# Moving the nine steps of the delta rule's inverses one row later in a hybrid decoder trunk

## The chip, the cores and the metric

The kernel runs on one core of a Trainium2 chip. A core has TensorE (matrix products, which write to PSUM), VectorE, ScalarE and GpSimd (elementwise work) and SyncE, whose queue issues the DMA transfers here. The metric is device time in microseconds; a time is the median of several runs, and one more execution is recorded by the hardware profiler. In the profile's rows PE is TensorE, PEld its weight loads, DVE VectorE, ACT ScalarE, POOL GpSimd and SPq the queue of SyncE.

## The reference

Two decoder layers over 512 tokens of width 1024, in float32. Each layer normalises x, projects it once, and feeds three branches: a Mamba-2 state space scan (SSD), multi-head latent attention (MLA) and a gated delta rule (GDN). Each branch is projected to the model width and multiplied by a sigmoid gate made from the same normalised x; the sum goes through an output projection, and a squared-ReLU feed-forward block follows.

```
g_ssd, g_mla, g_gdn = jnp.split(gates, N_BRANCH, axis=-1)
mixed = g_ssd * (y_ssd @ w_ssd_out) + g_mla * (y_mla @ w_mla_out) + g_gdn * (y_gdn @ w_gdn_out)
h = x + mixed @ w_out
f = jnp.square(jax.nn.relu(rmsnorm(h, norm2_g) @ w_up)) @ w_down
```

The delta rule has 8 value heads in chunks of 64 tokens. Each chunk and head needs the solution of a unit lower triangular system, which is what "the inverses" are:

```
a_mat = jnp.where(strict, jnp.einsum('bhcld,bhcmd->bhclm', kb, k) * decay, 0.0)
sol = lax.linalg.triangular_solve(a_mat + jnp.eye(L, dtype=jnp.float32), rhs, left_side=True, lower=True)
```

## The kernel before

**Products.** A float32 product is made of three matmuls in a faster format: each operand is split into a high part and the remainder. For weights, `split_half` casts the raw tile to `whi` on ScalarE (L154) and subtracts on VectorE to get `wlo` (L155); `mm3` issues the three matmuls (L182 to L184). Raw weights arrive by DMA into two buffers `wraw` (L161), issued by SyncE; `whi` and `wlo` have four buffers each.

**Rows.** `dense_F` makes 256 columns of a projection of K = 1024. Its weights come in four pieces, each of two 128-deep slices by 256 columns. One piece gives twelve matmuls of 128x512 (two output tiles, two slices, three matmuls each) into two of four PSUM banks `acc`. Such a piece is called a row here. Behind each row `dense_F` calls the function `after`, if it was given one.

**The state space projection.** `out_proj` goes through four pairs of output tiles. For each pair it makes the gate product (four rows on `xh`, `xl`, the normalised input) and the branch product (four rows on `yh`, `yl`). The projection of the state space branch is `out_proj(a["w_ssd_out"][ly], 0, ...)`; it has 32 rows, counted 0 to 31 here. Its `after` is `between`, which counts the rows and, from a given number on, runs one of a list of steps behind each row. The same `between` is also given to the query product (`key_tiles` in `gdn_unit`, four rows), so that steps left over run there: these are the counts 32 to 35 for the first unit.

**The inverses.** The 128x128 blocks of the delta rule for two units of four heads (tiles `nt`, tag `tok`) are made by `gdn_matrix`. Then:

- `gdn_blocks` inverts the 32x32 diagonal blocks on VectorE in 31 dependent pairs of operations (L879, L880), transposes the result (L882), writes both forms to memory (`d_x`, `d_y`, L885) and reads them back in another layout into the tiles `wk0` to `wk3` (L888: `wk<-d_x` for both units, then `wk<-d_y` for both). It is written ahead of the projection, and its VectorE work runs while the projection's early rows run on TensorE.
- `gdn_inverse` returns nine steps that put the inverses together: `first(0)`, `first(1)`, `second(0)`, `second(1)` and `last_doubling(0)` to `last_doubling(4)`. `first(u)` copies the block inverses (L907, L908 on ScalarE) and issues 64 small matmuls of 32x32 (L913), which read the tiles `wk<-d_x`. `second(u)` has 96 small matmuls (L929, L930). `last_doubling(i)` has up to sixteen of 64x64 (L949 of one half, L951 of the half before), whose results VectorE and ScalarE copy (L954, L956). Each step needs the copies of earlier ones. The small products go to three PSUM banks `sm`.

`gdn_unit(u)` then makes queries (convolved by L687 on ScalarE and L691 on VectorE), values and gates of a unit, and runs the scan over the chunks, which is the first to read the finished inverses.

**Order.** Nothing waits by hand. The program is written as one sequence; a planner orders each engine's instructions by a simulated clock: of those whose data and buffers it believes to be there, the one written first goes first (some are raised by `tc.high_priority`). So an instruction may stand later in its engine's queue than where it was written, when the planner believes its data to be late. At run time each engine, and SyncE's queue, takes its instructions strictly in the planned order and waits on semaphores.

Of the kernel before, what the change touches and what calls it, by code (L numbers as in the profile page):

```python
# [55 lines left out]
def hybrid_kernel(ctx, tc, a, out, depth=2, taps=None):  # L56
# [294 lines left out]
    for ly in range(depth):  # L351
# [609 lines left out]
        def gdn_unit(u, kT, ork, cc, cd, Yt, yh, yl):  # L961
            hd0 = 16 + 4 * u
            qT = key_tiles(2 * u, between)
            pss = sm_bank()
            for i in range(2):
# [116 lines left out]
        steps = gdn_inverse([m[4] for m in mats], blocks)  # L1082

        rows = itertools.count()

        def between():
            if next(rows) >= 24 and steps:
                steps.pop(0)()

        out_proj(a["w_ssd_out"][ly], 0, *ys, br, after=between)  # L1090
        yg = hilo_tags(lp, "y")
        for u in range(2):
# [302 lines left out]
```

## Time and profile before

| what | us |
|---|---|
| median of three runs | 2314.41 |
| the three runs | 2310.45, 2318.05, 2314.41 |
| profiled execution, its own time | 2314.88 |
| span of the profiled execution | 2313.1 |
| TensorE busy | 2272.7 |
| VectorE busy | 1647.6 |
| ScalarE busy | 1200.5 |

The span goes from the first to the last instruction; the execution's own time also has what lies around it, 1.78 us here. The profile gives for each engine its busy time, for groups of instructions their count, mean duration and idle time before them with what ended it, and a chain of work followed back from the last instruction. Matmuls are pipelined: the printed duration of one overlaps the next, so the pitch from start to start says what one costs. The mean granted clock of TensorE was 0.998. Each of the two layers goes once through the stage of the change: the first near 500 us and the second near 1646 us in the trace.

### The profile page before, as it was taken

How to read it: one execution, taken by the hardware profiler on the slowest of the kernel's cores; microseconds unless marked ns; L12 is line 12 of the kernel's file. 1: busy time of each engine (PE TensorE's matmuls, PEld its weight loads, DVE VectorE, ACT ScalarE, POOL GpSimd, SP SyncE). 2: the span in 40 equal slices, each digit the busy share in tenths (PEclk: the TensorE clock that was granted, in tenths of full speed). 3: DMA queues.
4: the chain of work that ended last, by engine and by line, in shares of the span. 5: the costliest groups of instructions: out<-in, count | busy, mean ns of one | idle time of the engine just before them, and what ended most of it. 6: DMA issues, size and time to landing. Idle time of an engine off the chain costs nothing.

```text
span 2313.1 us, 32290 instructions
## 1 busy us (share of the span) xinstructions
PE 2272.7 (98%) x11810; PEld 1866.7 (81%) x11810; DVE 1647.6 (71%) x3256; ACT 1200.5 (52%) x2509; POOL 59.5 (3%) x74
## 2 busy tenths in 40 slices
PE   9999999999999999999999999999999999999998
PEld 8788787878887888888888887878788878888886
DVE  7777566876667768767867775668657668778668
ACT  6766644333443455554657666433334435645545
POOL 0000000000000000000000000000000000000000
PEclk9999999999999999999999999999999999999999
DMA  4223534452324243233122236334422241433231
GB/s 142 80 74 101 191 101 119 125 140 74 87 69 164 65 146 107 94 104 108 59 89 79 75 107 197 95 112 141 119 82 83 65 164 55 160 107 101 89 110 46
DMA packets 220032, 244.16 MB, mean 106 GB/s; under 512 B 34256, under 2 KB 172384, under 8 KB 219872
## 3 DMA queue, kind: packets, MB, share of 16 engines
q1 hardware_dynamic: 219872, 242.09, 34.1%
q8 instruction: 93, 1.52, 0.3%
q14 instruction: 67, 0.55, 0.1%
HBM read 225.60 MB, written 11.74 MB: 103 GB/s over the span
## 4 chain that ended last, share of the span: by engine, by line
PE 86%; DVE 8%; ACT 2%; DMA 2%; POOL 1%; issue 1%; SPq 0%; DVEq 0%; POOLq 0%; ACTq 0%
PE acc L182 22%; PE acc L183 21%; PE acc L184 21%; PE sm L184 2%; PE sm L183 2%; PE sm L182 2%; DVE wlo L155 2%; PE sm L752 1%; ACT whi L154 1%; DVE tok L880 1%; PE sm L650 1%; DVE gQ L879 1%; PE sm L1037 1%; POOL gms L259 1%; PE yt L666 1%
## 5 line engine op out<-in xcount | busy, mean ns | idle before, releaser
L155 DVE TENSOR_TENSOR wlo<-wraw,whi 128x512 fp32r<-128x512 f32 (+1 forms) x536 | 366.4, 687 | 345.7 <-ACT whi L154 337.8
L154 ACT CAST whi<-wraw 128x512 fp32r<-128x512 f32 (+1 forms) x536 | 330.1, 618 | 541.5 <-PE acc L183 374.4
L182 PE MATMUL acc<-xh,whi 128*128 128x512 f32 (+1 forms) x1344 | 522.3, 390 | 0.8 <-ACT xh L254 0.8
L184 PE MATMUL acc<-xh,wlo 128*128 128x512 f32 (+1 forms) x1344 | 522.9, 389 | 0.0
L183 PE MATMUL acc<-xl,whi 128*128 128x512 f32 (+1 forms) x1344 | 522.2, 389 | 0.3 <-DVE xl L255 0.3
L183 PEld LDWEIGHTS acc<-xl,whi 128*128 128x128 f32 x1344 | 253.0, 188 | 48.7 <-DVE xl L255 1.4
L182 PEld LDWEIGHTS acc<-xh,whi 128*128 128x128 f32 x1344 | 252.4, 188 | 49.1 <-ACT xh L254 1.5
L184 PEld LDWEIGHTS acc<-xh,wlo 128*128 128x128 f32 x1344 | 253.0, 188 | 47.5
L154 ACT CAST whi<-wr 128x512 fp32r<-128x512 f32 x168 | 104.3, 621 | 108.7 <-PE acc L183 47.7
L183 PE MATMUL acc<-yl,whi 128*128 128x512 f32 x384 | 151.6, 395 | 0.0
L182 PE MATMUL acc<-yh,whi 128*128 128x512 f32 x384 | 150.9, 396 | 0.0
L184 PE MATMUL acc<-yh,wlo 128*128 128x512 f32 x384 | 150.1, 391 | 0.0
L155 DVE TENSOR_TENSOR wlo<-wr,whi 128x512 fp32r<-128x512 f32 x168 | 113.7, 689 | 38.1 <-ACT whi L154 37.4
L691 DVE SCALAR_TENSOR_TENSOR ckl<-acc,pc,ckl 128x511 f32<-128x511 f32 (+2 forms) x168 | 120.4, 744 | 15.5 <-ACT ckl L687 8.2
L182 PEld LDWEIGHTS acc<-yh,whi 128*128 128x128 f32 x384 | 71.7, 188 | 16.0 <-ACT yh L254 1.7
L184 PEld LDWEIGHTS acc<-yh,wlo 128*128 128x128 f32 x384 | 72.2, 188 | 14.5
L183 PEld LDWEIGHTS acc<-yl,whi 128*128 128x128 f32 x384 | 72.3, 188 | 13.8
L183 PE MATMUL acc<-wlo,xh 128*128 128x512 f32 (+1 forms) x208 | 80.1, 385 | 0.0
L184 PE MATMUL acc<-whi,xl 128*128 128x512 f32 (+1 forms) x208 | 79.7, 384 | 0.0
L182 PE MATMUL acc<-whi,xh 128*128 128x512 f32 (+1 forms) x208 | 79.2, 382 | 0.0
L1145 DVE TENSOR_TENSOR h<-h,acc 128x512 f32<-128x512 f32 x120 | 77.2, 682 | 0.2 <-PE acc L184 0.2
L454 ACT ACTIVATE eE<-eE,cum 128x128 f32<-128x128 f32 x192 | 63.1, 390 | 24.5 <-DMA eE<-d_c 19.8
(453 smaller groups left out, 4557.2 us busy)
## 6 DMA issues: line engine op xcount, KB each, us to landing
wraw<-in_w_in_dram SPq DMA_DIRECT2D x144, 512.0 KB, 3.6
wraw<-in_w_up_dram SPq DMA_DIRECT2D x64, 512.0 KB, 3.6
wr<-in_w_down_dram SPq DMA_DIRECT2D x32, 1024.0 KB, 5.5
eE<-d_c SPq DMA_DIRECT2D x48, 256.0 KB, 4.2
wraw<-in_w_mla_out_dram SPq DMA_DIRECT2D x16, 512.0 KB, 3.4
eE<-d_e SPq DMA_DIRECT2D x32, 256.0 KB, 2.9
wraw<-in_w_ssd_out_dram SPq DMA_DIRECT2D x16, 512.0 KB, 3.3
wraw<-in_w_gdn_out_dram SPq DMA_DIRECT2D x16, 512.0 KB, 3.3
```

What stands on the lines that cost most here:

```text
L154: act.copy(hi, raw)
L155: dve.tensor_tensor(lo, raw, f32(hi), ALU.subtract)
L182: pe.matmul(o, ah, bh, start=start, stop=False, skip_group_check=more)
L183: pe.matmul(o, ah, bl, start=False, stop=False, skip_group_check=more)
L184: pe.matmul(o, al, bh, start=False, stop=stop, skip_group_check=more)
L259: pool.tensor_tensor(o, o, (exp if exp is not None else nhalf)[:, : o.shape[1]], ALU.pow)
L454: act.activation(o[:, i], o[:, i], AF.Relu, scale=-1.0, bias=cum[:, t, h0 + i : h0 + i + 1])
L650: pe.transpose(ps[:, n : n + P], pn[t][:, kb * P : (kb + 1) * P], ident)
L666: pe.matmul(o, v_h, th[:, c : c + w], start=kb == 0, stop=False)
L691: dve.scalar_tensor_tensor(acc[:, d:], ps[:, : S - d], taps_[3 - d], acc[:, d:], ALU.mult, ALU.add)
L752: pe.matmul(py[64 * i : 64 * i + 64, c * P : (c + 1) * P], xd[:, t, h * 64 : (h + 1) * 64], e2[h // 4][:, h % 4, :], start=True, stop=True)
L1145: dve.tensor_tensor(hs_, hs_, ps[t], op)
```

## The change

The number from which `between` takes a step is raised by one. Behind row 24 no step runs any more; `first(0)` is written behind row 25, and so on. Of the nine steps, seven are now written within the projection (rows 25 to 31) and the last two behind the first two rows of the first unit's query product (counts 32 and 33); before, eight were within it and one behind the first row of the query product. In both layers the same.

```
--- before.py
+++ after.py
@@ -1084,7 +1084,7 @@
         rows = itertools.count()
 
         def between():
-            if next(rows) >= 24 and steps:
+            if next(rows) >= 25 and steps:
                 steps.pop(0)()
 
         out_proj(a["w_ssd_out"][ly], 0, *ys, br, after=between)
```

More of the change, by code (lines that the diff above doesn't have):

```diff
@@ L1086, in between @@
         def between():
-            if next(rows) >= 24 and steps:
+            if next(rows) >= 25 and steps:
                 steps.pop(0)()
```

## The prediction

> **What bounds the kernel now.** The first view is the page: span, busy time by engine, the granted clock and the chain that ended last.
>
> ```profile
> span 2313.1 us, 32290 instructions
> ...
> PE 2272.7 (98%) x11810; PEld 1866.7 (81%) x11810; DVE 1647.6 (71%) x3256; ACT 1200.5 (52%) x2509; POOL 59.5 (3%) x74
> ...
> PE 86%; DVE 8%; ACT 2%; DMA 2%; POOL 1%; issue 1%; SPq 0%; DVEq 0%; POOLq 0%; ACTq 0%
> ```
>
> TensorE is busy for 98% of the span and carries 86% of the chain. Its whole idle time is 2313.1 - 2272.7 = 40.4 us, so an edit that neither adds nor removes TensorE work can gain at most what it takes out of those 40 us. The second view, TensorE's waits over the whole span, says where they are; I keep the first two rows.
>
> ```profile
> PE sm L1018 <- DVE tok L1015: 3.4, 8, 0.5
> PE sm L913 <- DMA wk<-d_x: 3.0, 2, 1.8
> ```
>
> The second row belongs to the steps that are moved: L913 is the first matmul of the first step, `wk<-d_x` is the load of the 32x32 block inverses. It waits twice, once in each layer, 3.0 us in all and the single longest there is 1.8 us. Third, the table by stage, cut at row 24 of the projection and behind row 34, in both layers (the columns after the window are its length, then busy us and instruction counts):
>
> ```profile
> core 0: us, PE busy (x) PEld busy (x) DVE busy (x) ACT busy (x) POOL busy (x), PEclk, DMA share, GB/s
> 497.30:542.00 44.70, 42.92 (x586) 34.32 (x585) 19.42 (x31) 18.91 (x32) 0.00 (x0) 1.00 0.46 118
> 1643.90:1688.00 44.10, 42.91 (x586) 34.32 (x585) 19.19 (x31) 18.80 (x32) 0.00 (x0) 1.00 0.46 118
> ```
>
> In these 44.7 and 44.1 us TensorE is idle for 1.78 and 1.19 us, which is exactly the waits of L913: there is no other gap in the stage. VectorE and ScalarE are each busy for less than half of it, and the clock is 1.00. What a change in this stage is worth is read from that one wait.
>
> **The wait, row by row.** The timeline of TensorE around it, layer 0 and then layer 1 (start, duration, engine, line, tile; the bracket is idle time and its releaser):
>
> ```profile
> 497.27 0.39 PE L182 MATMUL acc<-xh,whi 128*128 128x512 f32 x1
> ...
> 499.99 0.39 PE L182 MATMUL acc<-xh,whi 128*128 128x512 f32 x1
> ...
> 501.35 0.39 PE L182 MATMUL acc<-xh,whi 128*128 128x512 f32 x1
> 503.52 1.20 PE L913 MATMUL sm<-wk,tok 32*32 32x32 f32 x64 [1.78 <-DMA wk<-d_x]
> 504.65 0.50 PE L183 MATMUL acc<-xl,whi 128*128 128x512 f32 x1
> ...
> 505.68 0.40 PE L184 MATMUL acc<-xh,wlo 128*128 128x512 f32 x1
> 506.01 1.20 PE L913 MATMUL sm<-wk,tok 32*32 32x32 f32 x64
> 507.14 0.50 PE L182 MATMUL acc<-xh,whi 128*128 128x512 f32 x1
> ```
>
> ```profile
> 1647.96 0.39 PE L182 MATMUL acc<-xh,whi 128*128 128x512 f32 x1
> 1649.54 1.20 PE L913 MATMUL sm<-wk,tok 32*32 32x32 f32 x64 [1.19 <-DMA wk<-d_x]
> 1650.67 0.50 PE L183 MATMUL acc<-xl,whi 128*128 128x512 f32 x1
> ```
>
> A row is twelve 128x512 matmuls. Row 24 starts at 497.27 and row 25 at 499.99, so a row takes 2.72 us and a matmul 2.72/12 = 0.227 us from start to start (the printed 0.39 overlaps its neighbour). The step `first(0)` is written behind row 24, but it does not stand there: from 499.99 to 501.35 there are 1.36/0.227 = 6 pitches, seven matmuls of row 25, then the step, then the other five. The planner has already pushed it as far as its own clock believes the load to need; the chip needs longer. `first(1)` stands where it was written, behind row 25, and waits for nothing.
>
> The real loss is a little less than the idle time and the pitch would suggest. A step that does not wait starts 506.01 - 505.68 = 0.33 us behind the matmul before it. So the first step was due at 501.35 + 0.33 = 501.68 and at 1647.96 + 0.33 = 1648.29; it came 1.84 and 1.25 us later, 3.09 us together. That is the most which moving it can win.
>
> **What releases it, and whether that moves.** The chain of work in order of time, then SyncE's queue in layer 0:
>
> ```profile
> 494.59 0.11 DVE tok L880
> ...
> 495.09 4.86 DMA d_x<-tok
> 499.95 0.02 issue
> 499.97 3.51 DMA wk<-d_x
> 503.48 0.04 issue
> 503.52 1.20 PE sm L913 x64
> ```
>
> ```profile
> 1641.47 5.01 DMA d_x<-tok
> 1646.49 0.02 issue
> 1646.50 3.00 DMA wk<-d_x
> ```
>
> ```profile
> 494.62 0.37 SPq L161 DMA_DIRECT2D wraw<-in_w_ssd_out_dram  x1
> 495.09 0.45 SPq L885 DMA_DIRECT2D d_x<-tok  x1
> 495.90 0.34 SPq L885 DMA_DIRECT2D d_y<-tok  x1
> 499.97 2.27 SPq L888 DMA_DIRECT2D wk<-d_x  x2
> 502.54 2.49 SPq L888 DMA_DIRECT2D wk<-d_y  x2
> 505.12 1.17 SPq L161 DMA_DIRECT2D wraw<-in_w_ssd_out_dram  x1
> ```
>
> The last of the 62 VectorE operations of the inverses ends near 494.7, the result is written to memory (4.86 us) and read back (3.51 us), and 0.04 us later the step starts. Nothing in that chain is released by TensorE's rows 24 or 25, and none of it is moved by the edit: it issues no DMA in a step. So I hold the landing at 503.48 and 1649.50.
>
> **The change, part by part.** It adds and removes no instruction; each of the nine steps goes one row later.
>
> First, `first(0)` goes from behind row 24 to behind row 25. By the planner's clock it is ready in the middle of row 25; written behind row 25 it ranks after that row's matmuls, so I expect it exactly at the row's end, five matmuls later. Those five, now run behind the wait, run in front of it: 5 x 0.227 = 1.135 us per layer. The step is then due at 501.68 + 1.135 = 502.82 and at 1649.43. Both are still ahead of the possible starts 503.52 and 1649.54, so waits of 0.70 and 0.11 us remain and the whole 1.135 us counts, twice: 2.27 us.
>
> The Trainium skill ("TensorE: Matmul & The Clock Gate", section "Back-to-back issue gap") gives about 131 ns per matmul for a sustained stream of weight loads and 512-column matmuls. By that figure, an estimate, the five matmuls would cover 0.66 us, the gain would be 1.31 us and the time 2313.6 us. The trace does not agree for these matmuls: 0.227 us in the rows above.
>
> Second, the other eight steps each keep their matmuls, their two transitions in and out of a row, and their copies. I price this at nothing; it is covered by a full row of 2.72 us between two steps, where now only five matmuls (1.14 us) lie between the first two. If that cover were gone, a step would wait for one copy of the step before, about 0.6 us by the rows just below; I take zero, since the steps that already stand a row apart show no idle time in the table.
>
> Third, on ScalarE the copies of `first(0)` wait for the same load and hold what is queued behind them.
>
> ```profile
> 499.96 0.62 ACT L154 CAST whi<-wraw 128x512 fp32r<-128x512 f32 x1 [2.10 <-PE acc L183]
> 503.50 0.62 ACT L907 COPY tok<-wk 32x512 f32<-32x512 f32 x1 [2.92 <-DMA wk<-d_x]
> ...
> 505.89 0.61 ACT L154 CAST whi<-wraw 128x512 fp32r<-128x512 f32 x1
> ...
> 535.54 0.58 ACT L956 COPY tok<-sm 64x512 f32<-64x512 f32 x1 [0.68 <-PE sm L951]
> ...
> 542.57 0.69 ACT L687 ACTIVATE ckl<-acc,pc 128x512 f32<-128x512 f32 x1 [0.96 <-PE acc L184]
> ```
>
> A cast starts as row 24 ends at 499.96; there are four `whi` buffers, so it is the weight of row 28, three rows or 8.2 us ahead of use. Row 29's cast, which today follows the end of row 25 at 505.9, would become due at 502.7 and, held by L907, L908 and L917, come by about 505.4: 2.7 us late against 8.2 us in hand. Cost zero.
>
> Fourth, `last_doubling(3)` leaves the projection and stands behind row 32, `last_doubling(4)` behind row 33, the second row of the query product. The last copy (L956, 535.54 to 536.12 now) moves by one row less the gain, 2.72 - 1.14 = 1.6 us, to 537.7; the next ScalarE work of that product starts at 542.57 - 1.14 = 541.43. That leaves 3.7 us, so zero. Were it gone, the copies of the last two steps (0.58 each on ScalarE) would lie in the convolution's way, 1.16 us per layer. The matrices themselves are read only in the scan of the unit, behind the key, value and gate products.
>
> The sum against the profiled execution, 2314.88 us (span 2313.1 and 1.78 around it): 2314.88 - 2.27 = 2312.61. The median of the three runs is 0.47 lower, 2314.41, and a new time will be a median: 2312.1. The ends of the term are 0 (the step stays where it stands) and 3.09 (it waits no more).
>
> **The rivals.**
>
> The load lands earlier than now, or the step goes further back, and the wait vanishes. For it: only 0.70 and 0.11 us remain, and the read back took 3.51 us in layer 0 but 3.00 in layer 1, so it varies by half a microsecond. Against it: nothing shortens it on purpose. Then 3.09 is won: 2314.41 - 3.09 = 2311.3.
>
> The change does nothing: the planner puts the step by readiness and not by rank, and readiness is still seven matmuls into row 25. For it: it has already moved the step off its written place. Against it: `first(1)` stands exactly where it was written, so ranks are kept once data is there. Time 2314.4.
>
> Slower: SyncE's queue. Its order is planned too. If the weight load at 505.12 came ahead of the four L888 loads and was one that waits for the buffer of rows 28 and 29, L888 would stand behind it. The subtraction's mean, for the next sum, is in the page's groups:
>
> ```profile
> L155 DVE TENSOR_TENSOR wlo<-wraw,whi 128x512 fp32r<-128x512 f32 (+1 forms) x536 | 366.4, 687 | 345.7 <-ACT whi L154 337.8
> ```
>
> That buffer is free when row 29's cast and subtraction are done: row 25 ends at 502.7, plus 0.62 and 0.69, 504.0; with 0.37 for the issue, L888 starts at 504.4 and not at 499.97, the load lands 4.4 us later, at 507.9, and TensorE, due at 502.82, waits 5.1 us where it lost 1.84: 3.3 us more per layer, 6.6 for both, 2321.0. It decides from the point where L888 is issued 1.14 us later than today. Against it: the loads L888 are written ahead of the projection and rank ahead of its weights, and the edit touches neither.
>
> The Trainium skill (same page, "What's actually happening") has TensorE's clock fall to half after an idle window of about 3.4 us. Only the slow rival's wait is that long, and another 1.7 us per layer (half of one such window, an estimate) would then be added. No wait of this kernel shown here reaches it: behind 1.78 us the clock reads 1.00.
>
> **How the numbers follow.** The forecast has 0.58, the vanished wait 0.10, no effect 0.16, the queue 0.16 (a third of it in one layer alone, 2314.4 - 1.1 + 3.3 = 2316.6). 0.3% is 6.9 us, about what a measurement of this kernel tells from no change; even the largest gain, 3.09 us, is 0.13%. So "within 0.3%" holds nearly every case: 0.83. Slower has 0.12: two thirds of the queue's case, whose two-layer time lies at the bound and beyond it with any further delay, and a little scatter. Faster has 0.05, scatter alone: the three runs before reach from 2310.45 to 2318.05. The range goes 4 us below the forecast by that scatter, to 2308.0, and up to no effect with the upper scatter and the queue in one layer, 2319.0; the two-layer queue lies outside.
>
> **What would show it.** In TensorE's timeline, `first(0)` behind twelve matmuls of row 25, its bracket at about 0.6 us in layer 0 and next to nothing in layer 1; twelve matmuls between it and `first(1)`; `d_x` and `wk` transfers of the same lengths at the same places; the last L951 group behind the second row of the query product. TensorE's idle time in the two stage windows falls from 2.97 us by some 2.2. The prediction is wrong if the step still stands behind seven matmuls, if L888 is issued later than 5 us behind L885, or if a new wait stands at L929, L949 or L969.

## The result and the profile after

| | median, us | lowest to highest | runs |
|---|---|---|---|
| before, beside it on the same chip | 2314.57 | 2310.45 to 2319.77 | 15 |
| after | 2308.81 | 2307.74 to 2310.89 | 15 |

The ratio is 0.9977 with a 95% interval of 0.9970 to 0.9984: 5.8 us faster, 0.25%. That is inside the predicted range and inside the 0.3% taken as measurable, but the gain is 2.5 times the 2.27 us forecast, and more than the 3.09 us that the prediction called the most. The upper end of the runs moved more than the lower one: 8.9 us against 2.7.

The page of the changed kernel, the same three lines as before:

```profile
span 2309.1 us, 32294 instructions
...
PE 2271.6 (98%) x11810; PEld 1865.2 (81%) x11810; DVE 1647.1 (71%) x3256; ACT 1201.0 (52%) x2509; POOL 59.4 (3%) x74
...
PE 88%; DVE 6%; ACT 2%; POOL 1%; DMA 1%; issue 1%; SPq 0%; DVEq 0%; POOLq 0%; ACTq 0%
```

The work is the same; TensorE's idle time fell from 40.4 to 37.5 us, and its share of the chain rose from 86 to 88%. Among TensorE's waits, the row of L913 went from 3.0 us in two waits to 0.7 in one.

```profile
PE sm L1018 <- DVE tok L1015: 3.4, 8, 0.5
...
PE sm L913 <- DMA wk<-d_x: 0.7, 1, 0.7
```

The table by stage, cut at the same places (row 24 to behind row 34, both layers):

```profile
core 0: us, PE busy (x) PEld busy (x) DVE busy (x) ACT busy (x) POOL busy (x), PEclk, DMA share, GB/s
497.61:541.15 43.54, 42.80 (x585) 34.20 (x584) 19.27 (x31) 18.89 (x32) 0.00 (x0) 1.00 0.46 126
1641.47:1684.17 42.70, 42.70 (x585) 34.21 (x584) 19.06 (x31) 18.92 (x32) 0.00 (x0) 1.00 0.46 127
```

Idle time is 0.74 and 0.00 us where it was 1.78 and 1.19. The lengths of the windows can't be compared as they are, since each holds one matmul fewer than before (585 against 586). Between the starts of the same two matmuls, the first of row 24 and one behind the last step, the stage took 541.91 - 497.27 = 44.64 and 1688.15 - 1643.88 = 44.27 us before, and 541.20 - 497.58 = 43.62 and 1684.46 - 1641.46 = 43.00 us after. That is 1.02 and 1.27 us less, 2.29 together.

The two profiled spans differ by 4.0 us, and these starts say where: ahead of the first stage +0.31, first stage -1.02, between the stages (1641.46 - 541.20) - (1643.88 - 541.91) = -1.71, second stage -1.27, behind it -0.31. The -1.71 lies in code that the change does not touch. There, in the profile of before, stands this (windows view, the clock is the third number from the right):

```profile
1206.00:1209.40 3.40, 2.24 (x18) 1.87 (x18) 1.74 (x6) 1.50 (x4) 0.91 (x1) 1.00 0.36 117
1209.40:1212.80 3.40, 3.40 (x9) 2.62 (x9) 2.41 (x5) 1.76 (x4) 1.12 (x1) 0.51 0.00 0
1212.80:1216.20 3.40, 3.40 (x20) 2.93 (x20) 2.50 (x5) 1.56 (x4) 0.00 (x0) 0.99 0.27 65
```

For one slice of 3.4 us TensorE runs at half clock. Half of the slice, 1.7 us, is the most that it can lose by that. Ahead of the slice a matmul starts 0.28 us later in this profile than the same one in the profile after (1209.22 against 1208.94), and behind it 1.90 us later (1213.65 against 1211.75), so the slice cost 1.62 us. The prediction had only looked at the stage of the change, where the clock reads 1.00. The profile of after has such a stretch too, in another place ahead of the stage, so this pair of profiles alone can't show the 3.5 us that the gain has beyond 2.29:

```profile
64.40:67.80 3.40, 3.40 (x10) 2.72 (x10) 2.42 (x5) 1.55 (x3) 1.13 (x1) 0.50 0.00 0
```

The mechanism that was forecast is there. TensorE around the moved step, layer 0 and then layer 1:

```profile
502.79 0.39 PE L184 MATMUL acc<-xh,wlo 128*128 128x512 f32 x1
503.91 1.20 PE L913 MATMUL sm<-wk,tok 32*32 32x32 f32 x64 [0.73 <-DMA wk<-d_x]
505.04 0.50 PE L182 MATMUL acc<-xh,whi 128*128 128x512 f32 x1
...
507.71 0.39 PE L184 MATMUL acc<-xh,wlo 128*128 128x512 f32 x1
508.03 1.20 PE L913 MATMUL sm<-wk,tok 32*32 32x32 f32 x64
```

```profile
1646.67 0.39 PE L184 MATMUL acc<-xh,wlo 128*128 128x512 f32 x1
1646.99 1.20 PE L913 MATMUL sm<-wk,tok 32*32 32x32 f32 x64
1648.12 0.50 PE L182 MATMUL acc<-xh,whi 128*128 128x512 f32 x1
```

The step stands at the end of row 25, behind an L184 and ahead of an L182, with a full row of twelve before `first(1)`. The transfers and their issues, from the chain of work and from SyncE's queue in layer 0:

```profile
495.39 4.94 DMA d_x<-tok
500.33 0.02 issue
500.35 3.52 DMA wk<-d_x
503.87 0.04 issue
503.91 1.20 PE sm L913 x64
```

```profile
495.39 0.45 SPq L885 DMA_DIRECT2D d_x<-tok  x1
...
500.35 2.28 SPq L888 DMA_DIRECT2D wk<-d_x  x2
```

Both transfers have the lengths of before (4.86 and 3.51 us there), and the read back is issued 4.96 us behind the write. Nothing moved in the queue.

### The profile page after: what moved, and what is told of

Its sections match the earlier page's. It is cut to its first block, busy times and chain, and to the rows that moved or that the text cites. A ratio compares the mean times of both kernels' runs of the same rounds, so it can differ in the third digit from the quotient of the medians.

```text
span 2309.1 us, 32294 instructions
## 1 busy us (share of the span) xinstructions
PE 2271.6 (98%) x11810; PEld 1865.2 (81%) x11810; DVE 1647.1 (71%) x3256; ACT 1201.0 (52%) x2509; POOL 59.4 (3%) x74
## 4 chain that ended last, share of the span: by engine, by line
PE 88%; DVE 6%; ACT 2%; POOL 1%; DMA 1%; issue 1%; SPq 0%; DVEq 0%; POOLq 0%; ACTq 0%
PE acc L182 22%; PE acc L183 22%; PE acc L184 22%; PE sm L183 2%; PE sm L184 2%; PE sm L182 2%; DVE wlo L155 2%; PE sm L752 1%; PE sm L650 1%; ACT whi L154 1%; PE sm L1037 1%; POOL gms L259 1%; PE sm L761 1%; PE yt L666 1%; PE sm L630 1%
## 5 line engine op out<-in xcount | busy, mean ns | idle before, releaser
L182 PE MATMUL acc<-xh,whi 128*128 128x512 f32 (+1 forms) x1344 | 521.9, 390 | 0.8 <-ACT xh L254 0.8
L184 PE MATMUL acc<-xh,wlo 128*128 128x512 f32 (+1 forms) x1344 | 522.2, 389 | 0.0
L182 PEld LDWEIGHTS acc<-xh,whi 128*128 128x128 f32 x1344 | 252.3, 188 | 49.6 <-ACT xh L254 1.5
L184 PEld LDWEIGHTS acc<-xh,wlo 128*128 128x128 f32 x1344 | 252.8, 188 | 47.7
L182 PE MATMUL acc<-yh,whi 128*128 128x512 f32 x384 | 150.8, 396 | 0.0
L184 PE MATMUL acc<-yh,wlo 128*128 128x512 f32 x384 | 149.9, 390 | 0.0
L182 PEld LDWEIGHTS acc<-yh,whi 128*128 128x128 f32 x384 | 71.6, 188 | 16.1 <-ACT yh L254 1.7
L184 PEld LDWEIGHTS acc<-yh,wlo 128*128 128x128 f32 x384 | 72.2, 188 | 14.5
L184 PE MATMUL acc<-whi,xl 128*128 128x512 f32 (+1 forms) x208 | 79.6, 384 | 0.0
L182 PE MATMUL acc<-whi,xh 128*128 128x512 f32 (+1 forms) x208 | 79.2, 382 | 0.0
```

Source lines behind the costliest of these rows:

```text
L182: pe.matmul(o, ah, bh, start=start, stop=False, skip_group_check=more)
L184: pe.matmul(o, al, bh, start=False, stop=stop, skip_group_check=more)
```

## The experiments

Two theories stood against each other. **A**: the gain is the wait alone, 3.1 us at most, and the rest is scatter. **B**: the gain is the wait, and beside it stretches at half clock, which the wait sets off in some executions and which cost up to 1.7 us each. All ratios are against the kernel before, run in the same rounds on the same chip; three chips served. One chip carried the first four kernels below, one the next four, one the last two.

Beside the times I use the mean granted clock of each run, which is given to three digits. One stretch takes 0.5 x 3.41 / 2313 = 0.0007 from it. In the profiles that have no stretch while TensorE works it reads 0.999 (it falls behind TensorE's last matmul in every profile, which costs nothing); with one or two it reads 0.998, with two or three 0.997.

**The kernel before, once more.** No edit.

> The kernel before, unchanged, for a second profile and for the scatter of its runs. Theory A (the change won the wait and nothing else; the other 3 us of the measured 5.8 are chance): ratio 1.000, and the mean granted clocks of its runs fall like those of the changed kernel, two in three at 0.999 and one in three at 0.998. Theory B (the idle time before the first step, together with the 1.1 us of 32x32 matmuls behind it, throws TensorE to half clock for 3.4 us in some executions, 1.7 us each): ratio 1.000 too, but its clocks lie lower, 0.998 and 0.997 more often than 0.999, its times stand in steps of about 1.7 us from some 2310.5 up, and a profile may show a half-clock stretch right behind the first step.

2317.31 us (2312.56 to 2322.55, 11 runs) against 2315.73 of its 33 companions: 0.9999 [0.9990, 1.0008]. This profile shows what the first profile of before did not, TensorE in layer 0 around the same wait:

```profile
502.33 0.39 PE L182 MATMUL acc<-xh,whi 128*128 128x512 f32 x1
504.57 1.55 PE L913 MATMUL sm<-wk,tok 32*32 32x32 f32 x64 [1.85 <-DMA wk<-d_x]
506.06 0.80 PE L183 MATMUL acc<-xl,whi 128*128 128x512 f32 x1
506.65 0.63 PE L184 MATMUL acc<-xh,wlo 128*128 128x512 f32 x1
507.08 0.63 PE L182 MATMUL acc<-xh,whi 128*128 128x512 f32 x1
507.50 0.63 PE L183 MATMUL acc<-xl,whi 128*128 128x512 f32 x1
```

```profile
501.70:505.10 3.40, 1.55 (x38) 1.05 (x37) 0.59 (x1) 0.55 (x1) 0.00 (x0) 1.00 0.86 139
505.10:508.50 3.40, 3.40 (x50) 2.40 (x43) 0.70 (x1) 2.21 (x5) 0.00 (x0) 0.50 1.18 188
508.50:512.00 3.50, 3.50 (x75) 3.06 (x75) 3.04 (x6) 3.13 (x6) 0.00 (x0) 0.99 0.81 225
```

Same program, same wait (1.85 us, 1.78 in the first profile), but here the clock falls to 0.50 in the slice behind it: the pitch of the 128x512 matmuls is 0.43 us instead of 0.227, and the step itself takes 1.55 us instead of 1.20. The slice before has 1.55 us of TensorE work in 3.40, of which the last 0.53 us are 32x32 matmuls. A row of TensorE's waits does not show this loss, since TensorE is busy. There are two more such stretches in this execution, at 64.8 and 1211.7 us. The first profile of before has neither the one at 64.8 nor the one at 505. Against it, the same matmuls fall back by 1.53 us over the first (from 63.02 against 62.82 to 71.82 against 70.09) and by 1.45 over the second (from 504.57 against 503.52 to 510.67 against 508.17). The Trainium skill ("TensorE: Matmul & The Clock Gate", section "What's actually happening") has a free-running window of 3413 ns, behind an idle one of which the clock is half; length and value agree with these rows, but the window ahead was not idle here.

**The first step where it stood, the others one row later.** `first(0)` is called inside row 25, behind the six matmuls of its first output tile. The planner still put it behind seven, as in the kernel before, and its waits are those of before (1.82 and 1.28 us).

```
-            for ps, c in zip(pss, cols):
+            for n, (ps, c) in enumerate(zip(pss, cols)):
 ...
+                if after and n == 0:
+                    after(True)
 ...
+            if inside:
+                if done[0] == 25 and len(steps) == 9:
+                    filler(FILL[ly])
+                    steps.pop(0)()
+                return
+            done[0] += 1
-            if next(rows) >= 24 and steps:
+            if next(rows) >= 25 and steps:
```

with `FILL = (0, 0)`, so that `filler` issues nothing.

> The first step is written behind the first six matmuls of row 25, the other eight where the kernel before has them. The start of the step is held by the landing, so one matmul more lies behind it, 0.23 us per layer. Theory A: 0.0 to 0.5 us over the kernel before. Theory B: the same, with the same low clocks and the same scatter of 8 to 9 us as the kernel before.

2316.54 us (2312.31 to 2320.59): 1.0001 [0.9993, 1.0010]. Moving the other eight steps alone is worth nothing that this interval of some 2 us to either side can show, as the prediction's sum had it; the gain hangs on the first step's place. In this profile the wait of layer 1 (1.28 us) set off two stretches in a row:

```profile
1647.00:1650.40 3.40, 2.12 (x69) 1.84 (x69) 0.15 (x1) 1.97 (x4) 0.00 (x0) 1.00 1.22 194
1650.40:1653.80 3.40, 3.40 (x69) 2.58 (x68) 2.09 (x5) 2.31 (x5) 0.00 (x0) 0.50 0.99 183
1653.80:1657.20 3.40, 3.40 (x10) 2.63 (x9) 1.53 (x3) 2.33 (x4) 0.00 (x0) 0.50 0.66 224
```

**The same, with the wait filled.** Eight matmuls of 128x512 in layer 0 and five in layer 1, into a spare bank that nobody reads, stand ahead of `first(0)`: `FILL = (8, 5)` and

```
+        def filler(n):
+            if n:
+                spare = y_bank()
+                for _ in range(n):
+                    pe.matmul(spare, xh[0][:, :P], xh[0], start=True, stop=True)
```

> As the kernel with the step behind six matmuls, with filler matmuls of 128x512 that nobody reads issued into the wait: eight in layer 0 (8 x 0.227 = 1.8 us), five in layer 1 (1.1 us). The step still waits for the same landing. Theory A: the time of that kernel, within 0.5 us, because idle time is filled with work that buys nothing. Theory B: about 3 us less, near 2311.5, most clocks at 0.999, and a scatter of 3 us in place of 8, because TensorE is no longer idle there.

2313.69 us (2312.78 to 2318.40): 0.9990 [0.9981, 0.9999], 2.9 us below the kernel without filler on the same chip. The timeline of TensorE in both layers:

```profile
501.25 1.97 PE L1105 MATMUL yt<-xh 128*128 128x512 f32 x8
503.49 1.20 PE L916 MATMUL sm<-wk,tok 32*32 32x32 f32 x64 [0.27 <-DMA wk<-d_x]
...
1646.66 1.29 PE L1105 MATMUL yt<-xh 128*128 128x512 f32 x5
1648.07 1.20 PE L916 MATMUL sm<-wk,tok 32*32 32x32 f32 x64
```

In layer 0 the step starts no earlier than before (503.49 and 503.52), so the useless matmuls win nothing of the wait itself. By A the time should have stayed within 0.5 us. Of 11 runs, 6 have a mean clock of 0.999, where the kernel without filler has none; the means of the clocks are 0.99836 and 0.99700. By the means of the times the gain is 1.9 us and not 2.9, and the scatter of 3 us that B expected did not come (it is 5.6 us), so the size is uncertain. The direction is not: this is the run that tells A and B apart, and B holds. The two profiles say the same. Apart from the fillers, TensorE's order is the same in both but for one matmul beside the step in each layer, and the whole difference of their spans, 3.1 us, arises at the two stretches behind the step of layer 1: the same matmul starts 0.09 us apart ahead of them (1649.86 against 1649.77) and 3.07 behind them (1657.62 against 1654.55). That is 1.5 us for each stretch.

**The block inverses loaded before they are done.** The load reads a buffer that is ready early, so the kernel leaves out the right block inverses; the wait is gone and the steps stay behind row 24.

```
-                    sync.dma_start(c, d_[u].rearrange("h b i j -> (b i) h j"))
+                    sync.dma_start(c, d_n[u].rearrange("h b i j -> (b i) h j"))
```

> The steps stand as in the kernel before, but the tiles wk are loaded from d_n, which is written long before, in place of d_x and d_y: the inverses are then made of the wrong blocks (their result is left out), and the first step has nothing to wait for. Theory A: 3.1 us less than before, near 2311.4. Theory B: about 6 us less, near 2308.5, with the clocks and the narrow scatter of the changed kernel.

2311.96 us (2309.12 to 2313.25): 0.9982 [0.9974, 0.9991], 3.8 us, between the two expectations. L913 waits for nothing, and no run has a clock below 0.998. But the planner, too, knew of the early load and put the step elsewhere (62 of its 64 matmuls directly behind row 24), so it is not the one-factor run it was meant to be; of the size it decides nothing.

**The changed kernel again, and the threshold one further, one back.** Edits of the one number: 25, 26 and 23.

> The changed kernel, unchanged, on the same chip as the three below. Theory B (the wait is won, and with it the half-clock stretches that it set off): again about 5.8 us under before, ratio near 0.9975, and most of its runs without a half-clock stretch (mean clock 0.999) or with one (0.998), where those of before have two or more (0.997 and lower) in half of the executions. Theory A (the wait alone, the rest chance): 2.6 us under before, ratio 0.9989, with clocks like those of before.

> The steps begin one row later still, behind row 26. By the changed kernel's profile 0.73 us of the wait was left in layer 0 and nothing in layer 1, and a row is 2.7 us, so the wait is gone in both. Theory A: 0.7 us under the changed kernel. Theory B: 0.7 us under it too, and no half-clock stretch behind the first step any more; those that are left come from elsewhere (near 64 and 1210 us), so the clocks are the changed kernel's. A new wait in the query product from the last three steps would show as a longer time.

> The steps begin one row earlier than before, behind row 23. The planner still puts the first step behind seven matmuls of row 25, so the wait is that of before, and the next steps crowd behind it: four matmuls, the second step, four matmuls, the third. Theory A: the time of before, within 1 us (0 from the wait, up to a microsecond if the third step waits for a copy). Theory B: the stretch of idle time and small matmuls is longer and falls over a whole activity window more often, so more half-clock stretches: 1 to 3 us over before, clocks of 0.997 and lower in most runs.

| threshold | median, us | lowest to highest | ratio to before [interval] | wait of L913, both layers | runs by mean clock 0.999 / 0.998 / lower |
|---|---|---|---|---|---|
| 23 | 2317.74 | 2312.20 to 2324.00 | 1.0008 [0.9998, 1.0018] | 2.9 | 2 / 1 / 8 |
| 24 (before, 33 runs) | 2315.40 | 2311.75 to 2319.57 | 1 | 3.0 in the first profile | 5 / 10 / 18 |
| 25 (after) | 2311.05 | 2309.80 to 2314.36 | 0.9981 [0.9972, 0.9990] | 0.7 in the first profile | 8 / 2 / 1 |
| 26 | 2310.13 | 2309.12 to 2312.04 | 0.9978 [0.9969, 0.9987] | none | 6 / 5 / 0 |

The change repeats in a second session with 4.4 us. The 0.9989 that A expected of it lies just inside the interval, so here the clocks speak for B and not the time alone. One row further the wait is gone, and the median is 0.9 us lower, near the 0.7 us that was still there, though the two intervals overlap. One row back the planner holds the step at about the same place with the same wait, as its row among TensorE's waits shows:

```profile
PE sm L913 <- DMA wk<-d_x: 2.9, 2, 1.8
```

Its 2.3 us over before lie within the noise by the interval. What it shows besides is how little one profile tells: its own was taken in an execution with no stretch at either step (two elsewhere, at 11.7 and 1209.8 us), while 8 of its 11 runs had a clock of 0.997 or less.

Comparing runs of equal clock does not size the wait. On this chip the change is worth 1.9 us among the runs with 0.999 (medians of 5 and 8 runs) but 4.1 among those with 0.998 (10 and 2 runs): a step in the third digit is more than one stretch, and the groups are small. The size of the wait rests on the two profiles, 2.29 us. What the full medians show beyond it, 4.35 - 2.29 = 2.1 us here, is the part left for fewer stretches.

**Keeping the clock up elsewhere.** With the threshold at 26, three filler matmuls of 128x256 stand ahead of the transposes of the key latent, the place at 64 and 1210 us where stretches were left.

```
+            spare = y_bank()
+            for _ in range(LATENT):
+                pe.matmul(spare[:, :256], ident, tok[0], start=True, stop=True)
             for k in range(nk):
                 ps = sm_bank()
```

> Steps behind row 26, and three filler matmuls of 128x256 in float32 that nobody reads, ahead of the transposes of the key latent near 62 and 1207 us, where TensorE is idle for 1.1 us and has only small work for two more. They can start once the first of four token tiles is scaled. Theory B: the remaining half-clock stretches, which begin at 64 and 1210 us in the profiles, become rarer: 0 to 1 us under the kernel with the steps behind row 26, nearly all clocks 0.999. Theory A: the same time or up to 1 us more, because the fillers overrun the idle time.

2316.59 us (2315.57 to 2319.75): 1.0006 [0.9997, 1.0014], 6.5 us over the kernel without the fillers. A miss. Nine of 11 runs are at 0.999 against six without the fillers, which points to fewer stretches; but the fillers changed the planner's order behind them, and the same matmuls come some 4 us later in the attention of layer 0 and 4 more in that of layer 1. The idle time at the place itself is still 1.10 us: the fillers stand behind the wait and not in it, and they take 1.40 us themselves in each layer (63.93 to 65.33, 1209.64 to 1211.04). This profile also has a stretch at half clock in the attention of layer 1, at 1293.96 us, behind a wait of 1.69 us. What else in the attention lost time stays open.

**Only the first step moved.** `first(0)` goes to the end of row 25, directly ahead of `first(1)`; all others stay.

```
-            if next(rows) >= 24 and steps:
-                steps.pop(0)()
+            if next(rows) >= 25 and steps:
+                [steps.pop(0)() for _ in range(1 + (len(steps) == 9))]
```

> Only the first step goes a row later: it stands behind row 25, directly ahead of the second step, which stays, as do the other seven. Theory A (the wait alone, and half-clock stretches by chance): 2.3 us under before, as the changed kernel would be by its wait. Theory B, if small matmuls count as idle time for the clock: the wait is as short as in the changed kernel (0.7 us and nothing), but 2.3 us of 32x32 matmuls follow it without a break, together 3.0 and 2.3 us, so in layer 0 nearly as long as the 3.0 us of before; half-clock stretches stay more frequent than in the changed kernel, and the time lies between: 2 to 4 us under before. Theory B, if idle time alone counts: 4 to 6 us under before with the clocks of the changed kernel.

2312.43 us (2310.05 to 2315.97): 0.9984 [0.9975, 0.9993], 3.6 us. Most of the gain comes with this one step. Some of the wait is left: the second load lands later than the first, and `first(1)`, now without a row between, waits for it. In layer 0:

```profile
503.70 1.20 PE L913 MATMUL sm<-wk,tok 32*32 32x32 f32 x64 [0.68 <-DMA wk<-d_x]
505.35 1.20 PE L913 MATMUL sm<-wk,tok 32*32 32x32 f32 x64 [0.46 <-DMA wk<-d_x]
```

L913 waits 1.6 us in all instead of 3.0, which is near the 1.5 us between this kernel and the next one on the same chip. Of the runs 4 / 6 / 1 are at 0.999 / 0.998 / lower, hardly fewer than the next kernel's 4 / 7 / 0, so the clocks do not say whether the 32x32 matmuls count as idle time.

**Two rows further.** The threshold at 27.

> The steps begin behind row 27, the last four behind all four rows of the query product. No wait was left behind row 26, so both theories: the time of that kernel, 5 to 5.5 us under before (ratio 0.9977), within 0.5 us. A longer time would mean that the last steps now meet the convolution of the queries or the key tiles (up to 1.2 us per layer by their copies).

2310.97 us (2308.99 to 2312.21): 0.9975 [0.9966, 0.9984]. From 25 on the gain is a plateau: 0.9977 and 0.9981, then 0.9978, then 0.9975. The versions at 26 and 27 are at least as good as the change, and no measurement here separates the three.

**The count of stretches.** Two counts can be made. The first takes all runs with a clock on record, by their mean clock (those of the kernel before that ran beside the first result have none):

| | runs | 0.999 | 0.998 | 0.997 | lower | mean |
|---|---|---|---|---|---|---|
| before, three chips | 87 | 9 | 32 | 28 | 18 | 0.99732 |
| after, two sessions | 26 | 19 | 6 | 0 | 1 | 0.99865 |

The difference of the means, 0.00133, is 1.8 stretches of 0.00074, or 2.7 us at the 1.5 us that one cost; by the slope of time against clock among the 87 runs of before (1.71 us per 0.001) it is 2.3. The second count takes the profiles: the four kernels with the full wait (before twice, the first step inside row 25, threshold 23) show 1, 3, 2 and 2 stretches while TensorE works, 2.0 each; the seven with a short wait, none, or a filled one (after twice, filled, early load, 26, first step only, 27; the key latent kernel left aside) show 1, 0, 0, 0, 0, 1 and 0, 0.3 each. That is 1.7 fewer.

That the second count is so near the first is partly luck. Of the 8 stretches, only 3 lie behind the moved step. One lies at 11.7 us, one at 64.8 and three at 1209.4 to 1211.7. The last two places are the transposes of the key latent in layers 0 and 1: in each of these eleven profiles TensorE waits there for 1.10 or 1.16 us and then runs small matmuls, and the change does not touch that code. What differs is the place of the clock's steps. They come on a grid of 3.413 us, and the fall behind the last matmul, which every profile has, gives its place (in the first profile of before that fall, at 2308.54 us, is 322.0 times 3.413 us behind the stretch at 1209.45). In the six cases with a stretch, the last step of the grid lay 1.02 to 1.62 us ahead of the end of the wait; in the sixteen without, it lay at most 0.91 or at least 1.76 us ahead. I take it that these stretches come by chance in either kernel. What is left of the profiles' count, 3 stretches behind the step in four profiles against none in seven, bears out the effect but not its size.

The size rests on the clocks of the 113 runs, and where their stretches stood is open for all but the few that were profiled.

## Why the prediction was right and where it failed

- **The place of the step**: right. Twelve matmuls of row 25, then the step, then twelve to the next.
- **What remains of the wait**: 0.73 us in layer 0 against 0.70 forecast; nothing in layer 1 against 0.11, so the rival of the vanished wait came true there.
- **The gain in the stage**: 2.29 us between the same matmuls against 2.27. The five matmuls by 0.227 us were the right price. The figure of 131 ns from the Trainium skill ("TensorE: Matmul & The Clock Gate", section "Back-to-back issue gap"), which would have made it 1.31, did not hold. (The time of 2313.6 that the prediction gives for that case starts from 2314.88; from the median, like the forecast, it is 2313.1.)
- **The parts put at nothing**: right, as far as can be told. The eight other steps moved and the first left gave a ratio of 1.0001; in the profile after, no wait stands at L929, L949 or L969. ScalarE and the last step came as forecast, the last L951 group behind the second row of the query product with its copy at 537.54 (forecast 537.7), and the query's convolution at 541.85 (541.43):

```profile
536.36 1.14 PE L951 MATMUL sm<-tok,kt 64*64 64x64 f32 x16
```

```profile
537.54 0.58 ACT L956 COPY tok<-sm 64x512 f32<-64x512 f32 x1 [0.68 <-PE sm L951]
...
541.85 0.69 ACT L687 ACTIVATE ckl<-acc,pc 128x512 f32<-128x512 f32 x1 [0.96 <-PE acc L184]
```

- **The rivals**: the planner did not hold the step back, and SyncE's loads were issued 4.96 us behind the write, as before (4.88). Neither happened.
- **The step that failed**: "That is the most which moving it can win", 3.09 us, together with the sentence that set the clock aside: "No wait of this kernel shown here reaches it: behind 1.78 us the clock reads 1.00." Both were read from one execution in which the stage happened to keep its clock. In another execution of the same program the clock behind the same wait reads 0.50. The missing term of the sum is 2 to 3 us: about 1.8 half-clock stretches fewer per execution by 1.5 us each, worked out above from the clocks of 113 runs. With it the sum is -2.3 - 2.7 = -5.0 us against the measured -5.8 and -4.4. The same step failed in the bound that an edit "can gain at most what it takes out of those 40 us" of idle time: the two profiles of before are busy for 2272.7 and 2274.7 us with the same 11810 matmuls, so busy time too can hold a loss.
- **The scatter**: the runs of before, 2310.45 to 2318.05, were taken for noise and only used to widen the range. The clocks of these three runs are not on record, but in the 87 later runs of before the time follows the clock: the medians by mean clock, from 0.999 down to 0.996, are 2312.87, 2314.82, 2316.59 and 2318.68.
- **The range**: that it holds 2308.81 is luck in part. Its lower end was set by that scatter; the largest gain that the prediction allowed led only to 2311.3.

## What to carry to other kernels

A wait of TensorE of 1 to 2 us with small matmuls beside it should be priced twice: its length, and 1.5 us for the share of executions in which the clock falls behind it. One profile shows one execution: compare the mean clock of all runs before a stage is said to keep its clock, and take scatter that follows the clock as a cost to be explained. Small matmuls next to a wait did not protect the clock here; full ones that filled it did (useless work won 2.9 us by the medians, 1.9 by the means). But fillers cost their own time where they do not fall into the wait, and in a planned program they change the order behind them (6.5 us lost at the key latent).

## What the runs showed of the hardware

- An idle time of 1.10 to 1.85 us with small matmuls behind it (32x32 at the moved step; 128x128 and 128x1 at the key latent) is enough, in some executions, for TensorE's clock to fall to 0.50. The slices ahead of the quoted half-clock slices of before and of the kernel with the first step inside row 25 still had 1.55, 2.12 and 2.24 us of TensorE work in 3.40. The Trainium skill ("TensorE: Matmul & The Clock Gate", section "HAM oscillation — how this bites in real kernels") gives "no PE-idle gaps >~3.4µs" as the rule; measured, idle times of about a third of that set it off.
- One stretch of 3.41 us at half clock cost 1.45, 1.53 and 1.62 us by the starts of the same matmuls in two profiles; two in a row cost 3.0.
- The stretches stand on a fixed grid within an execution. In the second profile of before they begin at 64.81, 505.13 and 1211.70 us: 440.32 and 706.57 us apart, 129.0 and 207.0 times 3.413. Between executions the grid lies elsewhere (11.69 and 1209.77 in the kernel with threshold 23, 351.0 times 3.413 apart). At the key latent the place of the grid separates the 6 waits that were followed by a stretch from the 16 that were not (above), which is how the same wait can be cheap in one run and dear in the next.
- A stretch can be followed by a second at once (6.83 us at half clock in the kernel with the first step inside row 25), though TensorE was busy in the first.
